# Layer 1's down projections of ten of the eleven pairs in seven products, tokens on partitions, with h turned once early

## The chip, the cores and the metric

The kernel runs on one core of one Trainium2 chip. The metric is device time in microseconds (us) for one execution. TensorE (PE) does the matmuls, VectorE (DVE), ScalarE (ACT) and GpSimd (POOL) the elementwise work, SyncE (SP) issues most DMAs. Each engine has a queue of its own and takes its instructions in order. PSUM, where matmuls add up, has 8 banks of 128 partitions by 512 fp32 values.

## The reference, cut to what matters

A decoder trunk of two layers, 512 tokens by 1024 channels, fp32. Layer 0 is a Conformer convolution module and a SwiGLU FFN, layer 1 sliding-window attention and a SwiGLU FFN, and then comes a last RMSNorm. The change lies in layer 1's FFN and what follows it:

```python
def swiglu_ffn(x, w_up, w_down):
    gate, up = jnp.split(x @ w_up, 2, axis=-1)
    return (jax.nn.silu(gate) * up) @ w_down

h = h + swiglu_ffn(rmsnorm(h, norm_ffn[l]), ffn_w_up[l], ffn_w_down[l])
return rmsnorm(h, norm_final)          # after the last layer
```

`w_up` is 1024 x 5632 and `w_down` 2816 x 1024. The kernel cuts the 2816 hidden channels into eleven "pairs" of 256.

## The kernel before, in words

**Products in three terms.** Operands are held as a high and a low part in a rounded fp32 format (fp32r): hi is a copy, lo is source minus hi. `mm3` (L346 to L352) adds hi*hi, hi*lo and lo*hi, so a product of 128x128 weights with 512 columns is three matmuls. `split` (L507) makes the parts of an activation with an ACT copy (L508) and a DVE subtraction (L509). `split_weights` (L233) does the same for weights (cast L234 on ACT, subtraction L237 on DVE).

**The weight stream.** All weights come as chunks of 128 x 1024 fp32 (512 KB) in the order of `PLAN`, through 4 buffers named `raw`. `SLOTS` lists what is to be split: a chunk, or one of the seven blocks of a pair. `advance` (L264) keeps the split three slots ahead of the matmuls; `whi` and `wlo` have 4 buffers each.

**Up projections of layer 1.** h is kept with channels on partitions, tokens along columns. Pairs 0, 2, 4, 7 and 10 are "plain" (`plain_pair`, L737): four chunks, four banks, 96 matmuls of 512 columns. Pairs 1, 3, 5, 6, 8 and 9 (`SEVENS`) go by Strassen's algorithm in Winograd's form (`ffn_up7`, L767): the 2x2 blocks A (weights: output half by input half) and B (x: input half by token half) are multiplied in seven products in place of eight. S1 to S4 are sums of weight blocks, made on POOL by `seven_sources` (L241; adds L255 to L261), T1 to T4 sums of x, made once (`Rows.sums`, L721). A product is 24 matmuls of 256 columns; its bank is added into a tile `up` by ACT, DVE and POOL (L788 to L801). Then DVE scales by the norm (L805), ACT applies silu (L807), POOL multiplies gate and up (L809), and `split` makes `hid`.

**Down projections of layer 1.** For three pairs at a time (`HALVES1`), `down_group` (L527) multiplies `hid` with 512 columns of tokens moving, and DVE adds each bank into h (L592). Pairs 9 and 10 go another way, in the tail: for each block of 128 tokens a class `Block` (L1385) turns h on PE (8 transposes, L1393) into two banks, adds the down products on top with tokens on partitions (24 matmuls, L1403), and then squares (ACT, L1408), takes 1/rms (POOL, L1414), multiplies by the gain (DVE, L1417), scales (L1425, L1427) and stores.

**The order of the work.** The kernel is written as one program; a scheduler that runs at build time sets the order on each engine, and buffers are given out from pools. The order of before: up 0-2, down 0-2, up 3-5, down 3-5, up 6-8, down 6-8, up 9, up 10, tail.

Of the kernel before, what the change touches and what calls it, by code (L numbers as in the profile page):

```python
# [14 lines left out]
ALU = mybir.AluOpType  # L15
# [20 lines left out]
HALVES1 = ((0, 3), (3, 6), (6, 9))  # L36
LAST = (9, 11)
# [18 lines left out]
SEVEN_FIRST = ("A11 B11", "S1 T1", "S3 T3", "S2 T2", "A12 B21", "S4 B22", "A22 T4")  # L56

# [5 lines left out]
def order_of(layer, pair):  # L63
    return SEVEN_FIRST if pair == SEVENS[0] else SEVEN
# [5 lines left out]

def slot_plan(plan):

    slots = []
    for i, c in enumerate(plan):
        if c[0] != "up" or not by_seven(c[1], c[2]):
            slots.append((i, None))
        elif c[3:] == (0, 0):
            slots += [(i + (3 if n else 1), (c[1], c[2], n)) for n in range(7)]
    return slots


def chunk_plan():
# [28 lines left out]
    for part in HALVES1:  # L111
        ffn(1, *part)
    for pair in range(*LAST):
        plan.extend(ups(1, pair))
    for kp in range(*LAST):
        for g in range(2):
            plan.append(("down", 1, kp, g))
# [71 lines left out]
def hybrid_trunk(ctx: ExitStack, tc: tile.TileContext, xT, W, prm_in, wdw_in, sinks, relb, onehot, fin, lead, out):  # L189
# [51 lines left out]
    def seven_sources(layer, pair, n):  # L241

        name = order_of(layer, pair)[n].split()[0]
        if name[0] == "S":
            sums[name] = sums_pool[0].tile([P, 2, 4, P], F32, tag="sum", name=uid("sum"), bufs=4)
        out = []
        for which in range(2):
            a = {f"A{m + 1}{half + 1}": raws[AT["up", layer, pair, half, which]].rearrange("p (k m c) -> p m k c", k=4, m=2)[:, m]
                 for half in range(2) if n or not half for m in range(2)}
# [3 lines left out]
            s = {k: v[:, which] for k, v in sums.items()}  # L253
# [8 lines left out]
        return out or [sums[name].rearrange("p a k c -> p (a k c)")]  # L262

    def advance():  # L264
        u = stream["use"]
        load(SLOTS[min(len(SLOTS) - 1, u + SPLIT_AHEAD - 1)][0] + 1 + DMA_AHEAD - SPLIT_AHEAD)
        while stream["split"] < min(len(SLOTS), u + SPLIT_AHEAD):
# [16 lines left out]
            for e in range(2):  # L284
                split_weights(*(w[:, e * 512:(e + 1) * 512].rearrange("p (k c) -> p k c", k=4) for w in (hi, lo)), src[e])

    def get_seven(layer, pair, n):

        advance()
        u = stream["use"]  # L290
        stream["use"] += 1
        assert SLOTS[u][1] == (layer, pair, n)
        return tuple(x.rearrange("p (a k c) -> p a k c", a=2, k=4) for x in splits.pop(u))
# [255 lines left out]
    def ffn_part(layer, part, xg, tok, rms, on_h=None, twin=False, plain=None):  # L549
        lo, hi = (HALVES0, HALVES1)[layer][part]  # L550
        hid = ffn_up7(layer, lo, hi, xg, pool7) if layer else ffn_up(layer, lo, hi, xg, tok, rms, twin, plain)
# [148 lines left out]
    class Hidden(Pairs):  # L700

        def __init__(self):
            self.per, self.q = 2, []

        def grow(self):
            self.q.append(quads.tile([P, 2, 2, 512], F32R, tag="quad", name=uid("hid")))

    class Rows:
# [12 lines left out]
        def sums(self):  # L721
# [4 lines left out]
            t1 = self.pool.tile([P, 2, 4, P], F32, tag="sum", name=uid("t1"), bufs=4).rearrange("p a k c -> p (a k c)").rearrange(  # L726
# [10 lines left out]
    def plain_pair(layer, pair, rows, hid, i):  # L737
        banks = accs(512)
        steps = None
        for half in range(2):  # L740
            for which in range(2):
                w = get("up", layer, pair, half, which)
# [14 lines left out]
        rs_bc = rows.rms.step2()  # L757
        hid.grow()
        for m in range(2):
            t1, t2 = temp(), temp()  # L760
            nc.vector.tensor_mul(t1, banks[m], rs_bc)
            nc.scalar.activation(t1, t1, AF.Silu)
            nc.vector.tensor_mul(t2, banks[2 + m], rs_bc)
            nc.gpsimd.tensor_mul(t2, t1, t2)
            split(hid[i + m], t2)

    def ffn_up7(layer, lo, hi, rows, pool):  # L767
        hid = Hidden()
        rms = rows.rms
        for pair in range(lo, hi):  # L770
            if not by_seven(layer, pair):
                plain_pair(layer, pair, rows, hid, 2 * (pair - lo))
                continue

            c = pool.tile([P, 2, 2, 2, 256], F32, tag="up", name=uid("up"), bufs=2)
            c11, c12, c21, c22 = (c[:, m, s] for m in range(2) for s in range(2))
            acc = {}
            for n, name in enumerate(order_of(layer, pair)):
                w = get_seven(layer, pair, n)
                a, b = name.split()  # L780
                x = rows.block[b]
                r = acc[a] = bank().rearrange("p (a s) -> p a s", a=2)
                for which in range(2):
                    for k in range(4):
                        mm3(r[:, which], [v[:, which, k, :] for v in w], [x[e][:, k, :] for e in range(2)],
                            which == 0 and k == 0, which == 1 and k == 3)
                if a == "A11":
                    nc.scalar.copy(c11, r)  # L788
                elif a == "S1":
                    nc.scalar.copy(c22, r)  # L790
                elif a == "S2":
                    nc.vector.tensor_add(c12, r, c11)
                    nc.vector.tensor_add(c21, acc["S3"], c12)
                    nc.gpsimd.tensor_add(c12, c12, c22)
                    nc.gpsimd.tensor_add(c22, c21, c22)
                elif a == "A12":
                    nc.vector.tensor_add(c11, r, c11)
                elif a == "S4":
                    nc.vector.tensor_add(c12, r, c12)
                elif a == "A22":  # L800
                    nc.vector.tensor_add(c21, r, c21)  # L801
            rs_bc = rms.step2().rearrange("p (s q) -> p s q", s=2).unsqueeze(2).to_broadcast([P, 2, 2, 256])
            hid.grow()
# [7 lines left out]
        return hid  # L811
# [560 lines left out]
    for part in range(len(HALVES1)):  # L1372
        ffn_part(1, part, nxt, ALL, None)

    hid = ffn_up7(1, *LAST, nxt, pool7)
    seven.close()

    res = ctx.enter_context(tc.tile_pool(name="res", bufs=2))  # L1380
    gain = res.tile([P, D], F32, tag="gain", name="gain", bufs=1)
    nc.sync.dma_start(gain, fin.to_broadcast([P, D]))
    chunks = {}

    class Block:  # L1385
        def __init__(self, b):
            self.b, self.tok = b, slice(b * P, (b + 1) * P)
            self.banks = [bank(), bank()]
            self.ss = small.tile([P, 4], F32, tag="ss", name=uid("ss"))
            self.hg = []  # L1390
            for i in range(KT):
# [40 lines left out]
    for kp in pairs:  # L1432
        for g in range(2):
            for bl in first:
                bl.down(kp, g)
                if kp == LAST[1] - 1:
                    bl.half(g)
# [36 lines left out]
```

## Time and profile before

| | us |
|---|---|
| runs before: median of 3 | 1076.69 |
| lowest, highest | 1074.96, 1078.26 |
| profiled execution, span from first to last instruction | 1073.4 |
| layer 1's FFN in it (first plain pair to the last store) | 724 to 1073 |
| down projections of three pairs, one stage | 32.6 |
| up pair, plain / seven products | 21.8 / 20.15 |
| last matmul to the end | 5.6 |

No time is listed for the profiled execution apart from its span. Rows of groups read: line, engine, operation, out<-in, shapes, count | busy us, mean ns of one | idle time before them and who ended it. Rows of timelines read: start us, length us, engine, line, operation. Rows of the chain: start us, length us, what.

### The profile page before, as it was taken

Reading aid. Unit: us, or ns where it says so; the run is one execution under the profiler, and the core shown is the slowest. Engines: PE = TensorE matmul, PEld = TensorE weight load, DVE = VectorE, ACT = ScalarE, POOL = GpSimd, SP = SyncE. Lnnn points to the kernel's source line nnn. Section 1 sums busy time; section 2 is a strip of 40 time slices with the busy share of each in tenths; the row PEclk is TensorE's granted clock in tenths of the full one; section 3 lists DMA queues with packets and bytes.
Section 4 is the critical chain, followed back from the end, with each engine's and each line's share of the span. In section 5 each row is a group of like instructions: output and inputs, shape, how many; then the busy total and the mean of one; then the engine's idle time right before and its main releaser. Section 6 shows DMA issues by size and latency. Waiting matters only on the chain.

```text
span 1073.4 us, 15809 instructions
## 1 busy us (share of the span) xinstructions
PE 1064.6 (99%) x5938; PEld 925.8 (86%) x5938; DVE 722.7 (67%) x1107; ACT 523.6 (49%) x943; POOL 434.7 (40%) x487
## 2 busy tenths in 40 slices
PE   9999999999999999999999999999999999999997
PEld 8888889999988888888888777779889898998986
DVE  3999988977777644443446566589756874866553
ACT  3887888765555333222342655475324342342333
POOL 3999998710322212111111353147352743635120
PEclk9999999999999999999999999999999999999999
DMA  9238045565555422222222211121522231324122
GB/s 353 88 100 97 2 154 200 180 233 180 182 187 191 145 98 97 99 98 98 98 87 93 76 59 66 55 77 40 177 98 79 79 138 59 138 79 137 66 73 78
DMA packets 39559, 124.45 MB, mean 116 GB/s; under 512 B 4251, under 2 KB 10556, under 8 KB 39484
## 3 DMA queue, kind: packets, MB, share of 16 engines
q1 hardware_dynamic: 38764, 122.36, 34.6%
q10 hardware_dynamic: 720, 1.10, 0.3%
q8 instruction: 46, 0.75, 0.3%
q14 instruction: 29, 0.24, 0.1%
HBM read 118.20 MB, written 5.24 MB: 115 GB/s over the span
## 4 chain that ended last, share of the span: by engine, by line
PE 96%; issue 1%; ACT 1%; DVE 1%; DMA 1%; SPq 0%; POOLq 0%; POOL 0%; DVEq 0%
PE bank L350 22%; PE bank L352 22%; PE bank L351 22%; PE bank L860 10%; PE bank L382 5%; PE bank L348 4%; PE bank L383 3%; PE bank L1403 2%; PE bank L1257 1%; PE bank L1299 1%; PE bank L1286 1%; PE bank L958 1%; PE bank L848 1%; DMA both<-in_lead_dram 1%; ACT quad L724 0%
## 5 line engine op out<-in xcount | busy, mean ns | idle before, releaser
L237 DVE TENSOR_TENSOR wlo<-raw,whi 128x1024 fp32r<-128x1024 f32 (+1 forms) x198 | 265.3, 1348 | 185.3 <-ACT whi L234 185.0
L351 PE MATMUL bank<-quad,whi 128*128 128x512 f32 (+1 forms) x1008 | 349.2, 346 | 1.0 <-DVE quad L505 1.0
L352 PE MATMUL bank<-quad,wlo 128*128 128x512 f32 (+1 forms) x1008 | 349.5, 347 | 0.0
L350 PE MATMUL bank<-quad,whi 128*128 128x512 f32 (+1 forms) x1008 | 349.4, 348 | 0.0
L234 ACT CAST whi<-raw 128x1024 fp32r<-128x1024 f32 (+1 forms) x198 | 190.3, 970 | 267.3 <-PE bank L351 209.4
L351 PEld LDWEIGHTS bank<-quad,whi 128*128 128x128 f32 x1008 | 191.1, 190 | 24.5 <-DVE quad L505 1.4
L350 PEld LDWEIGHTS bank<-quad,whi 128*128 128x128 f32 x1008 | 191.1, 190 | 24.5 <-issue 1.3
L352 PEld LDWEIGHTS bank<-quad,wlo 128*128 128x128 f32 x1008 | 191.0, 190 | 23.6 <-issue 0.6
L902 POOL TENSOR_TENSOR pr<-pr,pr 128x256 f32<-128x256 f32 x208 | 156.3, 782 | 6.7 <-ACT pr L901 6.7
L909 DVE SCALAR_TENSOR_TENSOR bank<-apad,wdw,bank 128x256 f32<-128x256 f32 x248 | 112.5, 485 | 3.4
L901 ACT ACTIVATE pr<-apad,wdw 128x256 f32<-128x256 f32 x208 | 98.2, 502 | 14.7 <-POOL pr L902 12.7
L860 PE MATMUL bank<-quad,w 128*128 128x256 f32 x448 | 98.7, 380 | 0.0
L860 PEld LDWEIGHTS bank<-quad,w 128*128 128x128 f32 x448 | 85.1, 190 | 11.7 <-DVE bank L909 0.2
L461 POOL TENSOR_TENSOR tmp<-tmp,tmp 128x256 f32<-128x256 f32 (+1 forms) x28 | 26.7, 955 | 123.1 <-ACT tmp L457 86.4
L382 PE MATMUL bank<-quad,whi 128*128 128x512 f32 x212 | 75.9, 398 | 0.0
L634 POOL TENSOR_TENSOR tmp<-tmp,tmp 128x512 f32<-128x512 f32 x12 | 17.2, 1432 | 112.0 <-DVE tmp L633 112.0
L237 DVE TENSOR_TENSOR wlo<-sum,whi 128x1024 fp32r<-128x1024 f32 x24 | 34.9, 1456 | 37.2 <-ACT whi L234 37.2
L383 PE MATMUL bank<-quad,wlo 128*128 128x256 f32 x212 | 59.4, 281 | 0.0
L351 PE MATMUL bank<-hid,whi 128*128 128x512 f32 x144 | 56.1, 390 | 0.0
L352 PE MATMUL bank<-hid,wlo 128*128 128x512 f32 x144 | 56.1, 389 | 0.0
L350 PE MATMUL bank<-hid,whi 128*128 128x512 f32 x144 | 55.8, 390 | 0.0
L352 PE MATMUL bank<-rows,wlo 128*128 128x256 f32 x192 | 54.4, 284 | 0.0
(211 smaller groups left out, 1617.0 us busy)
## 6 DMA issues: line engine op xcount, KB each, us to landing
raw<-in_W_dram SPq DMA_DIRECT2D x198, 512.0 KB, 3.6
w<-in_W_dram SPq DMA_DIRECT2D x14, 512.0 KB, 8.6
fd<-fs SPq DMA_DIRECT2D x1, 3072.0 KB, 33.5
h<-in_xT_dram SPq DMA_DIRECT2D x8, 256.0 KB, 8.5
bias<-fd SPq DMA_DIRECT2D x8, 256.0 KB, 5.0
both<-in_lead_dram SPq DMA_DIRECT2D x3, 512.0 KB, 6.3
out_dram<-hg SPq DMA_DIRECT2D x4, 256.0 KB, 2.0
out_dram<-hg ACTq DMA_DIRECT2D x4, 256.0 KB, 2.3
```

Source lines behind the costliest of these rows:

```text
L234: on_act = nc.scalar.copy(hi, src).ins
L237: latest[:] = [on_act, lo_engine[0].tensor_sub(lo, src, f32(hi)).ins]
L348: nc.tensor.matmul(out, w[0], x, start=start, stop=stop)
L350: nc.tensor.matmul(out, w[0], x[0], start=start, stop=False)
L351: nc.tensor.matmul(out, w[0], x[1], start=False, stop=False)
L352: nc.tensor.matmul(out, w[1], x[0], start=False, stop=stop)
L382: nc.tensor.matmul(first[2], first[0], first[1], start=start, stop=False)
L383: nc.tensor.matmul(second[2], second[0], second[1], start=False, stop=stop)
L860: mm = nc.tensor.matmul(self.pb[:, w * W2:(w + 1) * W2], w1_of(ct, w, k), x[k] if x else xg[k][:, tok], start=k == 0, stop=k == KT - 1)
L901: on_act = nc.scalar.mul(pr, a[:, j:j + W2], tap(j))
L902: on_pool = nc.gpsimd.tensor_add(pr, acc, pr)
L909: on_dve = nc.vector.scalar_tensor_tensor(yt if i == nd - 1 else c, src, tap(i), c if i else self.shift, op0=ALU.mult, op1=ALU.add)
```

## The change

**Down projections by seven products.** Ten pairs (0 to 9) are taken two at a time, in a "low" stage: A is `w_down` (two halves of the 1024 output columns, by the two 128-channel halves of a pair), B the hidden activations (two channel halves by two token halves). The order of stages is `STEPS1`: up 0, 1, 2, low 0, up 3, 4, low 2, up 5, 6, low 4, up 7, 8, low 6, up 9, 10, low 8, then pair 10's own down projection in the tail. So seven-product up pairs stand right ahead of low 4 (pair 6), of low 6 (pair 8), and next to each other (5, 6).

**Tokens on partitions.** The stationary operand is now a 128x128 piece of the activations, and 512 columns of weights move. One product is 12 matmuls (two token blocks, two pairs, three terms). Products add up in PSUM along three chains, `x` (A11, S2, S3, A22), `z` (S1, S4) and `y` (A12), each of two banks that are read after every product and then added to further.

**h turned once.** `flip` transposes h between the seven products of pair 1 (32 transposes on PE, 8 copies on ACT); h holds tokens on partitions from there on. The norm's scale is applied per token when a bank is added into h, so `up` is no longer scaled and DVE scales the gate alone.

**Forms.** `forms_of` makes from a pair's gated activations the four blocks B11, B12, B21, B22 and T1 to T4 (four POOL subtractions of 128x256, in place) and splits seven eighths of 2048 columns (1792) with two ACT copies and two DVE subtractions. Odd pairs keep the low part in the pool `form`, since 11 `quad` buffers would not do.

**The tail** has 12 matmuls a block for 32 matmuls and transposes; DVE scales the bank and adds h to it first, into an SBUF tile `room`, and the square and the gain work from there.

**Others.** In plain pairs DVE multiplies gate and up (POOL before). Down weights get S1 to S4 on POOL as the up weights do. `dynamic_dma_scratch_size` is 2048.

```diff
+LAST = FT // 2 - 1
+STEPS1 = [("up", 0), ("up", 1), ("up", 2), ("low", 0)]
+for _p in range(3, LAST, 2):
+    STEPS1 += [("up", _p), ("up", _p + 1), ("low", _p - 1)]
+SEVEN_LOW = ("A11 B11", "S1 T1", "S2 T2", "A12 B21", "S3 T3", "S4 B22", "A22 T4")
+def lows(pair):
+    return [("down", 1, kp, g) for g in range(2) for kp in (pair, pair + 1)]
...
-            rs_bc = rms.step2().rearrange("p (s q) -> p s q", s=2).unsqueeze(2).to_broadcast([P, 2, 2, 256])
-            hid.grow()
-            for m in range(2):
-                nc.vector.tensor_mul(c[:, m], c[:, m], rs_bc)
-                gate = c[:, m, :, 0, :]
-                nc.scalar.activation(gate, gate, AF.Silu)
-                t = temp()
-                nc.gpsimd.tensor_mul(t.rearrange("p (s q) -> p s q", s=2), gate, c[:, m, :, 1, :])
-                split(hid[2 * (pair - lo) + m], t)
+        rs_bc = rows.rms.step2().rearrange("p (s q) -> p s q", s=2)
+        for m in range(2):
+            gate = c[:, m, :, 0, :]
+            nc.vector.tensor_mul(gate, gate, rs_bc)
+            nc.scalar.activation(gate, gate, AF.Silu)
+            nc.gpsimd.tensor_mul(gate, gate, c[:, m, :, 1, :])
...
+    def forms_of(c, pool, odd):
+        f = c.rearrange("p m s w q -> p (m s w) q")
+        hi = quads.tile([P, 8, 256], F32R, tag="quad", name=uid("fhi"))
...
+        for t, a, b in (("T1", "B12", "B11"), ("T3", "B22", "B12"), ("T2", "B22", "T1"), ("T4", "B21", "T2")):
+            nc.gpsimd.tensor_sub(f[:, FORM[t]], f[:, FORM[a]], f[:, FORM[b]])
+        for part in (slice(0, 2), slice(3, 8)):
+            split((hi[:, part], lo[:, part]), f[:, part])
...
+    def low_pairs(pair, forms, rs):
+        chains = {}
+        for n, name in enumerate(order_of("low", pair)):
+            whi, wlo = get_seven("low", pair, n)
+            a, b = name.split()
+            chain, g, s = CHAINS[a]
+            first = chain not in chains
+            if first:
+                chains[chain] = [bank() for _ in range(2)]
+            for t, out in enumerate(chains[chain]):
+                for e in range(2):
+                    xh, xl = (f[:, FORM[b], t * P:(t + 1) * P] for f in forms[e])
+                    ws = slice(e * 512, (e + 1) * 512)
+                    for i, (x, w) in enumerate(((xh, whi), (xh, wlo), (xl, whi))):
+                        nc.tensor.matmul(out, x, w[:, ws], start=first and e == 0 and i == 0, stop=e == 1 and i == 2,
+                                         skip_group_check=True)
+                to, scale = rows_of(g, 2 * s + t), rs[:, 2 * s + t:2 * s + t + 1]
+                src = out.rearrange("p (i c) -> p i c", i=4)
+                if a == "A12":
+                    m = temp()
+                    nc.scalar.mul(m, out, scale)
+                    nc.gpsimd.tensor_add(to, to, m.rearrange("p (i c) -> p i c", i=4))
+                else:
+                    nc.vector.scalar_tensor_tensor(to, src, scale, to, op0=ALU.mult, op1=ALU.add)
...
+    def flip():
+        t, g = next(flips)
+        b = bank()
+        for i in range(4):
+            nc.tensor.transpose(b[:, i * P:(i + 1) * P], h[g * 4 + i][:, t * P:(t + 1) * P], ident)
+        nc.scalar.copy(rows_of(g, t), b.rearrange("p (i c) -> p i c", i=4))
...
+            nc.vector.scalar_tensor_tensor(v.rearrange("p (i c) -> p i c", i=4), acc.rearrange("p (i c) -> p i c", i=4), rs,
+                                           rows_of(g, b), op0=ALU.mult, op1=ALU.add)
+            nc.scalar.activation(temp(), v, AF.Square, accum_out=ss[:, g:g + 1])
```

More of the change, by code (lines that the diff above doesn't have):

```diff
@@ L252, in seven_sources @@
                 continue
-            s = {k: v[:, which] for k, v in sums.items()}
             if name == "S1":
@@ L1370, in hybrid_trunk @@
                 nxt = Rows("ffn1", pool7)
[L1372 to L1391, printed above, removed]
-                c = (i % 4) * P
-                nc.tensor.matmul(self.banks[i // 4][:, c:c + P], h[i][:, self.tok], ident, is_transpose=True,
-                                 start=i % 4 == 0, stop=False)
-        def down(self, kp, g):
-            if (kp, g) not in chunks:
-                chunks[kp, g] = get("down", 1, kp, g)
-            whi, wlo = chunks[kp, g]
-            for k in range(2):
-                a = cut(hid[2 * (kp - LAST[0]) + k], self.tok)
-                for n, (x, w) in enumerate(((a[0], whi), (a[0], wlo), (a[1], whi))):
-                    nc.tensor.matmul(self.banks[g], x, w[:, k, :], start=False, stop=kp == LAST[1] - 1 and k == 1 and n == 2)
-        def half(self, g):
-            ss, b = self.ss, self.banks[g]
-            sq = res.tile([P, 512], F32, tag="sq", name=uid("sq"))
-            nc.scalar.activation(sq, b, AF.Square, accum_out=ss[:, g:g + 1])
```

241 lines of the change are left out of this document (132 added, 109 removed).

## The prediction

> **What bounds the kernel now.** I read the page's busy times and chain first, then the chain in order of time, the groups of instructions, the busy time by stretch, and the timelines of VectorE (DVE) and GpSimd (POOL).
>
> ```profile
> span 1073.4 us, 15809 instructions
> ...
> PE 1064.6 (99%) x5938; PEld 925.8 (86%) x5938; DVE 722.7 (67%) x1107; ACT 523.6 (49%) x943; POOL 434.7 (40%) x487
> ...
> PEclk9999999999999999999999999999999999999999
> ...
> PE 96%; issue 1%; ACT 1%; DVE 1%; DMA 1%; SPq 0%; POOLq 0%; POOL 0%; DVEq 0%
> ```
>
> TensorE (PE) is busy 99% of the span, and 96% of the chain that ended last is PE. So fewer matmuls are worth their pace, as long as the other engines keep feeding PE. The pace is not the mean of a group:
>
> ```profile
> L351 PE MATMUL bank<-hid,whi 128*128 128x512 f32 x144 | 56.1, 390 | 0.0
> 1042.41 1.75 PE bank L1393 x16
> 1044.16 10.94 PE bank L1403 x48
> ```
>
> The first row (groups) gives 390 ns for a matmul over 512 columns, but matmuls overlap. In the chain, 48 of them take 10.94 us: 0.228 us each. I use 0.228; with 390 ns every saving would come out 1.7 times too large. The form of L1403 (activations stationary, 512 weight columns moving) is the one the new products use.
>
> ```profile
> 756.36:778.15 21.79, 21.79 (x99) 18.03 (x97) 15.02 (x15) 8.75 (x12) 6.34 (x5) 1.00 0.53 175
> 778.15:810.79 32.64, 32.64 (x146) 27.04 (x144) 17.33 (x17) 7.18 (x9) 13.77 (x9) 1.00 0.24 81
> 852.73:872.88 20.15, 20.15 (x169) 20.15 (x168) 15.61 (x17) 9.58 (x14) 5.03 (x3) 1.00 0.27 96
> ```
>
> These stretches are a plain up pair (21.79 us), the down projections of three pairs (32.64), and an up pair by seven products (20.15, so 2.88 a product). Columns: length, then busy PE, PEld, DVE, ACT, POOL, granted clock. PE has no idle time in any. The sums of a seven-product pair run on POOL in the stage before it (13.77 us in the down stage, 5.03 in its own).
>
> **What the change removes.** The order of instructions has 60 fewer 128x512 matmuls (2488 for 2548) and equal counts of every other form: two pairs' down projections take 84 for 96, five times. 60 x 0.228 = **13.7 us**. A low stage (that is what I call the seven down products of two pairs) lasts 84 x 0.228 = 19.15 us, a product 2.73. The 32 transposes move from the tail to pair 1 at the same price (1.75 / 16 = 0.11 each). Up to pair 1 of layer 1 all five queues stand in the same order.
>
> **What it adds beside PE.** A low stage splits 7 weight slots where the two pairs had 4, with 8 POOL sums of 128x512, 14 evacuations of a bank (12 on DVE, 2 on ACT and POOL) for 5.3, and for each pair 4 POOL differences of 128x256. Their prices:
>
> ```profile
> 842.26 1.78 DVE L509 TENSOR_TENSOR hid<-tmp,hid 128x512 fp32r<-128x512 f32 x1
> 843.97 2.31 DVE L237 TENSOR_TENSOR wlo<-sum,whi 128x1024 fp32r<-128x1024 f32 x1
> 846.20 0.68 DVE L761 TENSOR_TENSOR tmp<-bank,rsbc 128x512 f32<-128x512 f32 x1
> 859.69 1.23 DVE L237 TENSOR_TENSOR wlo<-sum,whi 128x1024 fp32r<-128x1024 f32 x1 [1.44 <-ACT whi L234]
> 1045.89 0.68 DVE L509 TENSOR_TENSOR hid<-tmp,hid 128x512 fp32r<-128x512 f32 x1
> ```
> ```profile
> 841.75 1.74 POOL L255 TENSOR_TENSOR sum<-raw,raw 128x512 f32<-128x512 f32 x1
> 843.45 1.74 POOL L261 TENSOR_TENSOR sum<-raw,sum 128x512 f32<-128x512 f32 x1
> 845.15 2.28 POOL L257 TENSOR_TENSOR sum<-sum,raw 128x512 f32<-128x512 f32 x1
> 847.51 1.30 POOL L261 TENSOR_TENSOR sum<-raw,sum 128x512 f32<-128x512 f32 x1
> L257 POOL TENSOR_TENSOR sum<-sum,raw 128x512 f32<-128x512 f32 x11 | 20.8, 1889 | 0.5
> L592 DVE TENSOR_TENSOR h<-bank,h 128x512 f32<-128x512 f32 x24 | 16.1, 686 | 6.1 <-PE bank L352 6.1
> ```
>
> A DVE operation with two SBUF inputs takes 0.68 us alone and 1.78 while POOL works; a POOL sum takes 1.30 alone and 1.74 to 2.28 beside DVE. They take turns: POOL starts every 1.70 us with a 512-wide DVE operation between, and a 1024-wide one stretches that to 2.36 (845.15 to 847.51). So 512 columns cost DVE about 0.6 of the turn and POOL 1.1. A DVE operation that reads a bank keeps 0.68 (L592: 686 ns over 24), so the 12 evacuations cost 0.69 each and take no turn; as scalar_tensor_tensor they are unmeasured at this width, and I let them be 0.6 to 0.8.
>
> In halves of 512 columns, then: a seven-product up stage has DVE 14 (weights) + 2 (gates) + 3.5 (splits of the forms) and POOL 8 + 2 + 2 + 2 (forms, halves of 256), so 19.5 x 0.6 + 14 x 1.1 = 27.1 us of turns in 20.15 us of PE. A low stage: 14 x 0.6 + 10 x 1.1 = 19.4 in 19.15. A plain pair: 11.5 x 0.6 + 2 x 1.1 = 9.1 in 21.8. The only place with two dear stages and no cheap one between is pair 5, pair 6, low 4 (73.6 in 59.5), and pair 8, low 6, pair 9 (73.6 in 59.5). Each is 14 over. Against that stand three weight slots made ahead (3 x 2.88 = 8.6) and the forms of its last pair, which can fall into the plain pair behind (2 x 1.1 + 3.5 x 0.6 = 4.3). So 1 us of stall at least in each, if the queues never stand in each other's way.
>
> The Trainium skill, page "SBUF — State Buffer", section "SBUF: two separate sides", has the same as a rule: DVE with two SBUF inputs and a reading GpSimd operation hold one port pair by turns, for a whole instruction. By it the 27.1 stands; by plain overlap the stage would need only 15.4 (POOL's part) and nothing would be over. The 1.70 us turns agree with the rule.
>
> **The path of low 4 and low 6.** Here the weights of a low stage follow a seven-product pair, whose raw chunks stay in use until its last product (A22) is split.
>
> ```profile
> raw<-in_W_dram SPq DMA_DIRECT2D x198, 512.0 KB, 3.6
> ACT whi L234 <- PE bank L351: 109.3, 49, 4.4
> L234 ACT CAST whi<-sum 128x1024 fp32r<-128x1024 f32 x24 | 25.1, 1046 | 50.6 <-PE bank L351 41.2 <-issue 8.2 <-POOL sum L255 1.2
> ```
>
> The casts wait for PE to free a buffer (109.3 us), so A22's split starts when PE ends the pair's S1 product; call that time 0. The split ends at about 2.4 (a cast of half a slot, 0.6, then DVE's 0.68 to 1.78), SP issues the chunks for row half 2, they land 3.6 later, at 6.0. S1 of the low stage needs them, and it is its second product. PE gets there after S2, A12, S4, A22 (4 x 2.88) and A11 (2.73), at 14.25. In POOL's built order S1 is complete with the 4th operation in low 4 and the 5th in low 6 (sums of S2 and S3 and an addition of the pair stand between), S2 four and five operations later. With 1.55 us an operation, between 1.30 and the 1.89 of L257, then 1.05 for the cast and 1.23 for DVE:
> - low 6: S1 at 6.0 + 7.75 + 2.3 = 16.05, PE stalls about 1.3 (two matmuls need the cast alone); S1 ends at 18.3; S2 is ready at 16.05 + 7.75 = 23.8; less four matmuls it can do first (0.9), a stall of 4.6.
> - low 4: S1 at 14.5, no stall; it ends at 17.0; S2 at 20.7, a stall of 2.8.
>
> Sum **8.7 us**. With 1.30 an operation it is 4.2, with 1.89 it is 15. Behind the waiting cast on ACT stand the next casts, and behind DVE's split the evacuations; both are in the sum. Low 0, 2 and 8 follow a plain pair, whose chunks come free one by one, three slots of 5.5 us ahead: nothing. Pair 1 gets 8 ACT copies for the turned h and needs 16 banks in 24 us: 0 to 3, I take 1.0 for this and small waits. Fewer scratch bytes for dynamic DMA: every queue of the page that moves a kernel's data is issued by SP or ACT, so 0. The load of the gains now stands on SP ahead of the last two chunks and waits for a matmul of pair 9, long past: 0.
>
> **The tail.**
>
> ```profile
> 1067.79 0.60 ACT L1408 ACTIVATE sq<-bank 128x512 f32<-128x512 f32 x1 [2.03 <-PE bank L1403]
> 1069.34 0.72 ACT L1427 ACTIVATE hg<-hg,rs 128x512 f32<-128x512 f32 x1 [0.85 <-POOL rs L1414]
> 1068.75 0.55 POOL L1414 TENSOR_TENSOR rs<-ss,mhalf 128x1 f32<-128x1 f32 x1 [5.78 <-DVE ss L1412]
> 1068.59 0.69 DVE L1417 TENSOR_TENSOR hg<-bank,gain 128x512 f32<-128x512 f32 x1
> 1069.39 0.48 DVE L1425 TENSOR_SCALAR hg<-hg,rs 128x512 f32<-128x512 f32 x1
> ```
>
> Now 5.6 us lie between the last matmul (1067.8) and the end: square, 1/rms, scale, store. The new tail puts a DVE operation (0.69) ahead of each square, and DVE has four operations of 0.6 and one of 0.4 a block, 3.0 us, for 12 matmuls of 2.7: it ends the tail. By its built order the last scale ends 4.2 us after the last matmul, then 3.3 as now: 7.5, **+1.9** (0.7 if only the one operation counts, 3 with waits).
>
> **Sum**, against the span of 1073.4, which lies 3.3 under the median 1076.69 of the runs; I carry the difference over: -13.7 + 8.7 + 1.0 + 1.9 = -2.1, so **1074.6 us**. About 3.2 us (0.3%) is what a measurement here can tell from no change.
>
> **Rivals.**
> - *The cover holds.* The sums run as fast as alone and raw chunks land early; stalls 0 to 4.2: 1064.9 to 1069.1, say 1067. For it: no PE idle in any stretch above, though turns are taken there too. Against it: no stage of before has sums due right behind a seven-product pair.
> - *The turns become the bound.* Half of the cover (12.9 in each place) is lost since the queues are in order: 28 - 13 = 15 of stall, and 4 where low 0 and low 2 meet pairs 3 and 5 (27.1 + 19.4 in 39.3, 7 over each): -13.7 + 1.9 + 19 = +7.2, 1084. It decides from 15 us of stall on. For it: L257 at 1.89 instead of 1.30. Against: four plain pairs that need 9.1 of 21.8.
> - *The clock drops.* In every slice PEclk is 9, and the stretches above have 1.00. If it halved for one product behind each stall, each would lose 2.73: 1080. The Trainium skill, "TensorE: Matmul & The Clock Gate", section "What's actually happening", halves it after an idle window of about 3.4 us; by that, an estimate, 1.7 would be lost in each place. No run here shows it.
> - *It does not do what it says*: excluded, the built order has the 60 matmuls less.
>
> **Chances.** Forecast 0.44 (1070 to 1079); cover holds 0.23; turns bound 0.27; clock 0.06. Faster by over 0.3%: 0.23 and a good third of the forecast (stalls under 7.6), 0.39. Within: 0.29. Slower: 0.27 and the clock, 0.32. The range reaches from inside the first rival to the second's price: 1066 to 1084; it leaves out the best of the one and the worst of the other.
>
> **What would show it.** PE's 128x512 matmuls 60 fewer at 0.228; low 0, 2 and 8 near 19.2 us, low 4 near 22 and low 6 near 25, with PE's idle time put down to the split (wlo) or cast (whi) of S2; POOL's mean sum over 1.5; a tail with DVE last. Wrong, if low 4 and low 6 last 19 to 20, or if stalls stand in low 0, 2 and 8 or inside the seven-product pairs.

## The result and the profile after

The changed kernel takes 1090.87 us (median of 4 runs, 1089.23 to 1091.58), the kernel before 1077.47 beside it (1074.96 to 1079.25). The ratio is 1.0125, with a 95% interval of 1.0108 to 1.0142: some 13 us slower. I had forecast 1074.6, at most 1084. The profiled run of the changed kernel took 1090.52, with a span of 1088.7, against a span of 1073.4 before. A run lasts 1.8 us longer than its span, so 1073.4 answers to some 1075.2, one of the short runs of before; that is why the spans lie 15.3 us apart and the medians 13.4.

The page of the changed kernel, the lines that answer to those shown of before:

```profile
span 1088.7 us, 15932 instructions
...
PE 1063.3 (98%) x5878; PEld 920.5 (85%) x5878; DVE 778.2 (71%) x1181; ACT 554.5 (51%) x991; POOL 544.4 (50%) x567
...
PEclk9999999999999999999999999989999998999999
...
PE 86%; POOL 5%; DVE 4%; issue 2%; ACT 1%; DMA 1%; SPq 0%; POOLq 0%; DVEq 0%; ACTq 0%
```

Two things are new. PE has 60 matmuls fewer (5878 for 5938), but is hardly less busy (1063.3 for 1064.6 us), and PEclk, which was 9 everywhere, has slices of 8. And POOL and DVE now hold 9% of the chain, where before POOL had 0% and DVE 1%.

The stretches in which PE runs the first 72 matmuls of each low stage, in the order low 0, 2, 4, 6, 8 (busy PE, PEld, DVE, ACT, POOL, then granted clock):

```profile
786.50:803.14 16.64, 16.64 (x75) 13.73 (x74) 15.27 (x20) 7.85 (x11) 10.42 (x10) 1.00 0.38 127
847.71:864.35 16.64, 16.64 (x75) 13.72 (x74) 14.78 (x19) 7.85 (x11) 11.03 (x10) 1.00 0.37 128
911.07:936.14 25.07, 20.63 (x75) 15.18 (x74) 19.46 (x22) 10.58 (x14) 21.85 (x15) 0.86 0.20 63
980.63:1003.80 23.17, 18.78 (x76) 14.52 (x75) 19.94 (x18) 10.54 (x15) 22.67 (x16) 0.93 0.24 72
1049.71:1066.36 16.65, 16.65 (x74) 13.73 (x73) 15.18 (x22) 8.76 (x12) 3.74 (x2) 1.00 0.17 64
```

Low 0, 2 and 8 run at 16.64 / 72 = 0.231 us a matmul (0.229 from one start to the next), with no idle time. Low 4 and low 6 take 8.4 and 6.5 us more. In low 4 PE is idle for 25.07 - 20.63 = 4.4 us, and nearly all of the rest is the clock (0.86). POOL, busy for 10 to 11 of 16.6 us in low 0 and 2, is busy for 22 of 25.1 and of 23.2 us in low 4 and 6.

The waits of PE from layer 1's FFN on, in the changed kernel (us in total, times, longest):

```profile
PE bank L857 <- ACT whi L244: 7.7, 3, 3.7
PE bank L857 <- DVE wlo L247: 1.1, 2, 0.7
PE bank L857 <- DVE h L866: 1.1, 1, 1.1
PE bank L368 <- ACT whi L244: 1.0, 1, 1.0
PE bank L369 <- DVE quad L523: 1.0, 1, 1.0
PE bank L370 <- DVE wlo L247: 0.8, 1, 0.8
PE bank L489 <- DVE tmp L479: 0.5, 1, 0.5
```

L857 is a low product: 9.9 us of waits, all in low 4 (4.4) and low 6 (5.5). L368 and L370 are products of up pair 6, 1.8. The lines with quad L523 and tmp L479 stand in before as well (1.0 and 0.5). So 11.7 us of new waits.

The stretches of the changed kernel in which the clock is halved (the clock is the third number from the end of a row):

```profile
725.39:732.22 6.83, 6.83 (x21) 5.67 (x21) 6.83 (x5) 2.09 (x2) 6.13 (x4) 0.50 0.16 30
899.47:902.88 3.41, 3.41 (x18) 3.41 (x17) 3.41 (x3) 3.06 (x5) 3.33 (x3) 0.50 0.00 0
916.53:919.94 3.41, 2.96 (x7) 2.17 (x7) 2.25 (x4) 0.00 (x0) 3.41 (x3) 0.50 0.00 0
923.36:926.77 3.41, 3.38 (x9) 2.07 (x8) 3.41 (x4) 2.56 (x4) 3.33 (x3) 0.50 0.00 0
991.63:995.04 3.41, 3.02 (x7) 2.44 (x8) 3.41 (x4) 1.44 (x2) 3.41 (x3) 0.50 0.14 22
```

They last 3.41 us or twice that, and each of the last four stands behind a wait: in pair 6, twice in low 4, and in low 6. At half the clock 3.41 us do the work of 1.7. The first lies behind two holes (1.0 and 0.5 us) near pair 0 that the kernel before has too.

The sum of the profiled runs, 15.3 us between the spans:

| | us |
|---|---|
| 60 matmuls fewer, 0.228 each | -13.7 |
| waits in pair 6, low 4, low 6 | +11.7 |
| four halved windows behind them, 1.7 each | +6.8 |
| the halved window near pair 0 | +3.4 |
| tail, 8.7 us after the last matmul (1080.0) for 5.6 | +3.1 |
| layer 0 and attention, where nothing was changed | +1.75 |
| left over | +2.3 |

Of the left over, 0.9 is the pace: from one start to the next a low product's matmul takes 0.229 us, one of the old down projections 0.227, over 420 of them. The rest wasn't followed further. The 1.75, and the halved window near pair 0, differ from trace to trace: that window is halved in 9 of the 14 traces of this study and not in 5, with the same two holes in all.

### The profile page after: what moved, and what is told of

Same layout as the page of the kernel before. It is cut to its first block, busy times and chain, and to the rows that moved or that the text cites. A ratio compares the mean times of both kernels' runs of the same rounds, so it can differ in the third digit from the quotient of the medians.

```text
span 1088.7 us, 15932 instructions
## 1 busy us (share of the span) xinstructions
PE 1063.3 (98%) x5878; PEld 920.5 (85%) x5878; DVE 778.2 (71%) x1181; ACT 554.5 (51%) x991; POOL 544.4 (50%) x567
## 4 chain that ended last, share of the span: by engine, by line
PE 86%; POOL 5%; DVE 4%; issue 2%; ACT 1%; DMA 1%; SPq 0%; POOLq 0%; DVEq 0%; ACTq 0%
PE bank L368 17%; PE bank L369 17%; PE bank L370 17%; PE bank L915 10%; PE bank L857 6%; PE bank L400 5%; PE bank L366 4%; PE bank L401 3%; DVE wlo L247 2%; PE bank L1312 1%; PE bank L1354 1%; PE bank L1341 1%; POOL sum L270 1%; POOL sum L272 1%; PE bank L1013 1%
## 5 line engine op out<-in xcount | busy, mean ns | idle before, releaser
L247 DVE TENSOR_TENSOR wlo<-raw,whi 128x1024 fp32r<-128x1024 f32 (+1 forms) x208 | 259.3, 1257 | 156.5 <-ACT whi L244 156.0
L368 PE MATMUL bank<-quad,whi 128*128 128x512 f32 (+1 forms) x1008 | 350.5, 349 | 0.0
L370 PE MATMUL bank<-quad,wlo 128*128 128x512 f32 (+1 forms) x1008 | 349.9, 347 | 0.0
L244 ACT CAST whi<-raw 128x1024 fp32r<-128x1024 f32 (+1 forms) x208 | 186.6, 912 | 234.0 <-PE bank L369 169.2
L368 PEld LDWEIGHTS bank<-quad,whi 128*128 128x128 f32 x1008 | 191.9, 190 | 24.9 <-issue 1.6
L370 PEld LDWEIGHTS bank<-quad,wlo 128*128 128x128 f32 x1008 | 191.5, 190 | 24.0 <-issue 0.6
L247 DVE TENSOR_TENSOR wlo<-sum,whi 128x1024 fp32r<-128x1024 f32 x44 | 64.7, 1470 | 37.1 <-ACT whi L244 37.0
L479 POOL TENSOR_TENSOR tmp<-tmp,tmp 128x256 f32<-128x256 f32 (+1 forms) x28 | 26.7, 954 | 123.3 <-ACT tmp L475 86.6
L244 ACT CAST whi<-sum 128x1024 fp32r<-128x1024 f32 x44 | 46.0, 1047 | 83.2 <-POOL sum L270 48.1
L857 PE MATMUL bank<-whi,fhi 128*128 128x512 f32 x140 | 53.7, 405 | 8.8 <-ACT whi L244 7.7
L857 PE MATMUL bank<-wlo,fhi 128*128 128x512 f32 x140 | 57.4, 410 | 1.2 <-DVE wlo L247 1.1
L1331 POOL TENSOR_SCALAR sc<-sc,sm 128x256 f32<-128x256 f32 (+1 forms) x64 | 31.2, 506 | 52.9 <-DVE sm L1329 52.6
```

Of the source, the lines that this page charges most:

```text
L244: on_act = nc.scalar.copy(hi, src).ins
L247: latest[:] = [on_act, lo_engine[0].tensor_sub(lo, src, f32(hi)).ins]
L368: nc.tensor.matmul(out, w[0], x[0], start=start, stop=False)
L370: nc.tensor.matmul(out, w[1], x[0], start=False, stop=stop)
L857: nc.tensor.matmul(out, x, w[:, ws], start=first and e == 0 and i == 0, stop=e == 1 and i == 2, skip_group_check=True)
```

## Experiments

Two theories stood at first. The **path**: the sums of a low stage come late, because a seven-product pair in front frees its raw chunks late (so the forecast put it). The **turns**: where two dear stages adjoin a low stage, DVE and POOL need the shared port for longer than PE's work lasts. And for the clock: it falls because PE is idle, or because of something else in the change.

**Seven-product pairs only ahead of plain ones.**

```diff
-SEVENS = (1, 3, 5, 6, 8, 9)
+SEVENS = (1, 3, 5, 7, 9)
```

> Five up pairs by seven products (1, 3, 5, 7, 9) in place of six, so that a plain pair stands ahead of every low stage and no two seven-product pairs adjoin. PE has 24 more matmuls of 512 columns for 168 of 256: 21.8 - 20.15 = +1.6 us. In the changed kernel PE waited 1.8 us inside pair 6, 4.4 in low 4 and 5.5 in low 6, and the clock was halved four times for 3.41 us right behind those waits (6.8 us lost): 18.5 in all. Path theory (the sums of a low stage come late because its raw chunks are freed late by a seven-product pair) and turns theory (POOL and DVE have more turns than time where dear stages adjoin) both expect that all of it goes: about 1090.9 - 18.5 + 1.6 = 1074, and 1071 if the halved clock near pair 0 (3.4 us) goes as well. Rival (a low stage is too dear by itself, wherever it stands): waits of 4 us or more stay in low 4 and low 6, 1085 or more.

Measured 1071.15 us against 1076.4 before: 0.995 (0.9932 to 0.9969). PE from 940 to 1060 us of this kernel, the stretch in which low 6 and low 8 run (the latter but for its end), and all its waits from the FFN's first product on:

```profile
940.00:1060.00 120.00, 120.00 (x637) 103.75 (x635) 94.25 (x111) 51.32 (x74) 72.24 (x50) 1.00 0.28 93
```
```profile
PE bank L368 <- DVE tmp L775: 1.8, 1, 1.8
```

No wait in any low stage, and no halved window before PE's last matmul. The 1.8 is in pair 1. So a low stage isn't too dear by itself; what stands in front of it decides. Both theories expected that.

**Another order of the low products.** (One line: `SEVEN_LOW` = A11, A12, S1, S2, S3, S4, A22.)

> Order of the products of a low stage: A11, A12, S1, S2, S3, S4, A22, so A12, which needs no POOL sum, comes second and S1 third, one product (2.73 us) later. Path theory: the wait for S1 and S2 shrinks by 2.73 in low 4 (4.4 to 1.7) and in low 6 (4.4 to 1.7), and two or three halvings of the clock (1.7 each) go with it: about 1081. The wait inside pair 6 (1.8) stays. Turns theory: the amount of work on POOL and DVE is the same, so the wait comes at S2, S3 or later in the stage: 1088 to 1092.

Measured 1093.78 against 1076.4: 1.0158 (1.0139 to 1.0178), above the turns' range (1088 to 1092) and far from the path's 1081. The waits in low 4 and 6 stay (9.2 us by the profile), and 3.5 come up in the pair behind low 6. To be needed later didn't help: against the path.

**A12 on DVE alone.**

```diff
-                if a == "A12":
-                    m = temp()
-                    nc.scalar.mul(m, out, scale)
-                    nc.gpsimd.tensor_add(to, to, m.rearrange("p (i c) -> p i c", i=4))
-                else:
-                    nc.vector.scalar_tensor_tensor(to, src, scale, to, op0=ALU.mult, op1=ALU.add)
+                nc.vector.scalar_tensor_tensor(to, src, scale, to, op0=ALU.mult, op1=ALU.add)
```

> The two A12 banks of a low stage are added into h by DVE straight from the bank (0.74 us each) in place of an ACT copy (0.69) and a POOL addition of two SBUF operands (1.58): POOL loses 3.2 us a stage, DVE gains 1.5 that takes no turn on the port. Turns theory: the wait in low 4 and low 6 falls by up to 3 each, and behind it the clock: 1080 to 1086. Path theory: the additions of A12 stand behind S1 and S2 of their own stage, so less than 2 us of change, 1089 to 1091.

Measured 1088.94 against 1076.4: 1.0111 (1.009 to 1.0132), which overlaps the changed kernel's 1.0108 to 1.0142. Taken as forecast, this fits the path (1089 to 1091) and not the turns (1080 to 1086): POOL has 3.2 us less to do in a stage, and the waits in low 4 and low 6 are 10.7 us for 9.9. But the turns' figure had left out when the work falls. In the changed kernel POOL's two additions of A12 begin at 932.4 in low 4, behind its last wait (to 923.0), and at 1001.1 in low 6, behind the main one (to 990.1). So the run is inconclusive.

**The late chunks made those that need fewer sums.**

```diff
...
-    return [("down", 1, kp, g) for g in range(2) for kp in (pair, pair + 1)]
+    return [("down", 1, kp, g) for g in (1, 0) for kp in (pair, pair + 1)]
...
-SEVEN_LOW = ("A11 B11", "S1 T1", "S2 T2", "A12 B21", "S3 T3", "S4 B22", "A22 T4")
+SEVEN_LOW = ("S1 T1", "A11 B11", "S2 T2", "A12 B21", "S3 T3", "S4 B22", "A22 T4")
```

> Chunks of a low stage come with the second output half first (A21, A22, then A11, A12), and the products go S1, A11, S2, A12, S3, S4, A22. So the two chunks that come early are those S1 needs, and the late ones are needed by A11 (no POOL sum) and S2. Behind the late landing stand two POOL sums (S2) in place of four (S1, S2). Path theory: the wait in low 4 and low 6 falls by two POOL operations, 3 us each, and one or two halvings of the clock go: about 1081 to 1083. Turns theory: 1088 to 1092.

Measured 1090.21 against 1076.4: 1.013 (1.0109 to 1.0151), no gain, in the range of the turns. Low 6's waits fell to 1.8, low 4's rose to 6.1, and low 0 and low 8 got 1.8 and 1.4. Again the waits move and don't go.

**A shorter DVE operation in the place of the split.**

```diff
+        if seven:
+            nc.vector.tensor_copy(lo, f32(hi)[:, 0:1].to_broadcast(lo.shape) if len(lo.shape) == 2 else f32(hi)[:, :, 0:1].to_broadcast(lo.shape))
+            return
...
```

This kernel and the next leave out the low part of the weights in all slots of seven products.

> The changed kernel, but the low part of the weights of every seven-product slot is not computed: DVE writes the first column of the high part over all columns, so it reads one operand from SBUF in place of two; every other instruction stays. Turns theory (a DVE operation with two SBUF inputs and a POOL sum take turns on one port): POOL's sums go from a mean of about 1.7 to about 1.3 us, DVE's splits to their time alone, and the waits in pair 6, low 4 and low 6 and the halved clock behind them go: about 1090.9 - 18.5 = 1072. Rival (too many instructions on POOL and DVE, or late sums, whatever the port does): POOL's sums keep their 1.7, 1088 to 1092. If DVE's new operation turns out much shorter than 0.69 for 512 columns, it is POOL's own length that tells the two apart.

Measured 1073.51 against 1076.35: 0.9968 (0.9953 to 0.9983). The waits of PE are 3.9 us, and but for the window near pair 0 no window is halved. But POOL's own length, which was to tell the theories apart, lies in between. DVE's new operation and the dearest POOL sum (groups, from the FFN on):

```profile
L246 DVE CAST wlo<-whi 128x512 fp32r<-128x512 f32 x64 | 46.2, 742 | 13.3 <-ACT whi L244 12.4
```
```profile
L279 POOL TENSOR_TENSOR sum<-raw,sum 128x512 f32<-128x512 f32 x21 | 36.5, 1743 | 0.4
```

The copy takes 742 ns on average, though 410 at the least, and POOL's 82 sums still average 1.55 us: beside POOL, the copy with one SBUF operand is lengthened as well, and the sums with it, only less. The Trainium skill, page "SBUF — State Buffer", section "SBUF: two separate sides", counts DVE's two-port modes among those that lock the port pair. The lengthened copies fit that if the copy runs in such a mode, which no run here shows by itself. So this run doesn't tell the port from DVE's amount of work.

**DVE's splits off the port, and not shorter.**

```diff
+        if seven:
+            if not fixed:
+                fixed.append(bank())
+                nc.vector.memset(fixed[0], 0.0)
...
+                for j in range(src.shape[1] // 512):
+                    nc.vector.tensor_sub(lo[:, j * 512:(j + 1) * 512], f32(hi)[:, j * 512:(j + 1) * 512], fixed[0])
+            return
...
```

> The changed kernel, but the low part of the weights of every seven-product slot is not computed: DVE subtracts a PSUM bank of zeros from the high part, 512 columns at a time, so it has one operand in SBUF and one in PSUM, at the length of the evacuations (0.69 for 512, 1.38 in place of 1.21 for 1024). So DVE has as much work as before, a little more, but its splits leave the port. Turns theory: POOL's sums fall from a mean of 1.64 to at most 1.4, and the waits in pair 6, low 4 and low 6 and the halved clock go: 1072 to 1075, with up to 2 more since one bank is taken away. Rival (DVE's amount of work, not the port): POOL's sums keep 1.6, waits as before, 1088 to 1094.

Measured 1069.44 against 1076.26: 0.9941 (0.9927 to 0.9954), below the range of the turns theory. Splits and sums, from the FFN on, first of the changed kernel, then of this one:

```profile
L247 DVE TENSOR_TENSOR wlo<-raw,whi 128x512 fp32r<-128x512 f32 x64 | 60.4, 975 | 5.5 <-ACT whi L244 5.5
L247 DVE TENSOR_TENSOR wlo<-sum,whi 128x1024 fp32r<-128x1024 f32 x43 | 63.5, 1476 | 37.1 <-ACT whi L244 37.0
```
```profile
L276 POOL TENSOR_TENSOR sum<-raw,sum 128x512 f32<-128x512 f32 x21 | 39.0, 1859 | 0.5
L272 POOL TENSOR_TENSOR sum<-sum,raw 128x512 f32<-128x512 f32 x21 | 35.9, 1713 | 0.4
```
```profile
L255 DVE TENSOR_TENSOR wlo<-whi,bank 128x512 fp32r<-128x512 f32 x115 | 73.8, 681 | 34.6 <-ACT whi L246 34.0
```
```profile
L288 POOL TENSOR_TENSOR sum<-raw,sum 128x512 f32<-128x512 f32 x21 | 32.5, 1547 | 0.5
L284 POOL TENSOR_TENSOR sum<-sum,raw 128x512 f32<-128x512 f32 x21 | 27.9, 1330 | 0.5
```

A split of 512 columns takes 681 ns with an operand in PSUM (670 to 691 in all its places), where it took 975 on average and up to 1787 with both in SBUF. L284's sums fall from 1713 (then L272) to 1330 ns; the mean of all sums is 1.39 us for 1.64. DVE's work alone has not become less (two operations of 681 in the place of one over 1024 columns, which takes 1210 at the least). The waits in pair 6, low 4 and low 6 fall from 11.7 to 0.8 us, and no window is halved before the last matmul. The instructions on POOL are the same, with six seven-product pairs and all. One thing beside the port differs: raw chunks and POOL's sums come free earlier, since DVE doesn't read them. In the changed kernel POOL waited for no sum to be split between 860 and 1020 us, so the chunks are left. POOL's first sum of low 4 and of low 6 in this kernel (timeline, idle time in brackets):

```profile
897.32 1.94 POOL L282 TENSOR_TENSOR sum<-raw 128x512 f32<-128x512 f32 x1 [3.09 <-DMA raw<-in_W_dram]
959.49 1.29 POOL L282 TENSOR_TENSOR sum<-raw 128x512 f32<-128x512 f32 x1 [9.78 <-DMA raw<-in_W_dram]
```

Low 4 begins at 904.4 here and low 6 at 966.6. So in low 6 the first sum begins 7.1 us ahead of its stage, where in the changed kernel it was 6.3, after much the same wait for a chunk; even so PE's waits there fall from 5.5 to 0.2 us. In low 4 it begins 7.1 us ahead for 1.9, so there the earlier chunk can have a share. With that reserve for pair 6 and low 4, the turns on the port are the cause. The next run weighs the chunks alone.

**Five raw chunks.** (The pool of raw chunks has 5 buffers in place of 4, the odd pairs' low forms 7 blocks in place of 8, and `dynamic_dma_scratch_size` is 1024 for 2048.)

> The changed kernel with five raw chunks in place of four (room for it by cutting the unused eighth of the low forms). The third chunk of a low stage, the first that S1 needs, can then land before the seven-product pair in front ends; the fourth as before. If it matters that POOL waits for raw chunks at the border (3.0 us of idle time ahead of low 4, 1.4 ahead of low 6), the waits fall by 1 to 2 us in each place, and the time to 1086 to 1089. If the turns of POOL and DVE alone set them: 1090 to 1092.

Measured 1091.08 against 1076.26: 1.0137 (1.0123 to 1.015), no gain. The waits are 11.2 us, low 6's down to 2.4, with new ones in pairs 5 and 6. The first sum of low 4 now begins 15.2 us ahead of its stage, that of low 6 22.7. Then POOL waits for DVE instead: 5.2 and 4.0 us ahead of two sums of low 6, until DVE has split earlier ones. So a chunk more moves the waits and doesn't lessen them, and the path as forecast doesn't set their size. The fourth chunk of a stage came late here too (the second S1 sum begins 1.9 us ahead of low 4 and 4.1 ahead of low 6); six chunks had no room and weren't tried.

**The low stages' sums on DVE.** (The four lines of `seven_sources` go by `nc.vector` for low stages.)

> The S sums of the low stages (8 of 128x512 a stage) on DVE in place of POOL. Turns theory: 0.6 of the turn in place of 1.1 each, so 4 us less a low stage; what is over in each of the two places falls from 14 to 10, and the waits there by about half: 1080 to 1084. If POOL's amount of work alone were the bound, all waits would go: 1072. If DVE's own time becomes the bound (14 x 0.6 + 8 x 0.68 + 14 x 0.74 and more in 19.15 us), waits appear in low 0, 2 and 8 as well: 1090 or more.

Measured 1084.68 against 1076.35: 1.0081 (1.0052 to 1.011). Lower than the changed kernel by 0.4%, near 5 us, though the two intervals just touch: the way of the turns, but just above their range, and far from the 1072 for POOL's amount of work. Low 6's waits fell from 5.5 to 2.2. Those of low 4 did not (5.3).

**The adjoining pairs put elsewhere.** (`SEVENS` = 1, 3, 5, 7, 9, 10.)

> Pairs 1, 3, 5, 7, 9 and 10 by seven products: six again, but the one place where dear stages adjoin is now pair 9, pair 10, low 8. Turns theory: the waits of 4 to 6 us and one or two halvings of the clock (1.7 each) that stood in low 6 now stand in pair 10 or low 8, and nowhere else: the alternating kernel's 1071.2 - 1.6 + 6 to 9 = 1075.6 to 1078.6. Rival (adjoining does not matter, the stretch from pair 5 to low 6 was disturbed by something else): 1069.5.

Measured 1082.39 against 1076.35: 1.0057 (1.0036 to 1.0078). The waits of PE:

```profile
PE bank L857 <- ACT whi L244: 4.6, 2, 2.6
PE bank L857 <- DVE wlo L247: 1.8, 3, 0.6
PE bank L368 <- ACT whi L244: 1.0, 1, 1.0
PE bank L370 <- DVE wlo L247: 0.8, 1, 0.8
```

Low 4 and low 6 have none now. Low 8, which had none in the changed kernel, has 6.3, and pair 10 has 1.9; two windows are halved behind them. The place follows the adjoining pairs, at 8.2 us a place for the 4 to 6 that I had put down, which is why the time lies above the range. The path, too, would put waits behind pair 10, so this run speaks against the rival alone.

**Holes in the kernel before.**

```diff
+                if pair in HOLES and which == 0:
+                    x = rows.x[half * 4][0]
+                    for _ in range(HOLES[pair][half]):
+                        nc.vector.tensor_copy(x, f32(x))
...
```

In these pairs the order of the matmuls is changed as well, so that the chunks on both sides of a hole use the copied tile.

> The kernel before, with eight holes made on purpose in PE's work: in the plain pairs 2, 4, 7 and 10, between the two chunks of a half, DVE copies one activation tile onto itself 1, 2, 3, 4, 5, 2, 3 and 1 times (0.48 us each), and PE has to wait for it. Holes of about 0.5 + 0.48 n: 1.0, 1.5, 1.9, 2.4, 2.9, 1.5, 1.9, 1.0, some 14 us in all. Theory that idle time of PE halves the clock in the next window of 3.41 us when about 1.5 us of a window are idle: four to six halvings behind the longer holes, 1.7 us each: 1076.5 + 14 + 7 to 10 = 1097 to 1101. Rival (the halved clock of the changed kernel comes from something else in it): no halvings, 1090.

Measured 1092.79 against 1076.35: 1.0152 (1.0117 to 1.0187). Only two holes came about, in pairs 4 and 7, but long ones, 5.87 and 6.92 us, so the time lies below the range that stood for eight. Two stretches of this kernel, which begin inside the holes:

```profile
847.38:854.21 6.83, 5.08 (x12) 4.09 (x13) 4.86 (x8) 0.63 (x1) 1.32 (x1) 0.50 0.25 77
949.78:956.61 6.83, 3.12 (x7) 2.48 (x8) 6.00 (x8) 0.64 (x1) 2.28 (x2) 0.50 0.24 79
```

The clock, 1.00 in the kernel before, halves for 6.83 us at both, and nowhere else before the tail. So idle time of PE is enough; the change's own instructions aren't needed. The two places cost some 8.5 us each for holes of 5.9 and 6.9; part of each hole lies in the halved stretch itself. How long a short hole must be, this run can't say.

**The tail's gain on POOL**, with alternating pairs.

```diff
-            nc.vector.tensor_mul(o, v, gain[:, g * 512:(g + 1) * 512])
+            (nc.vector if g else nc.gpsimd).tensor_mul(o, v, gain[:, g * 512:(g + 1) * 512])
```

> The alternating kernel (pairs 1, 3, 5, 7, 9 by seven products), and in the tail POOL multiplies the first half of a block by the gain, so that DVE has 2.6 us a block in place of 3.3 against PE's 2.7. If DVE's backlog makes the tail's 8.7 us: the last addition of h follows the last matmul at once, and the time falls by 0.7 to 1.5, to 1069.7 to 1070.5. If the chain behind the last matmul (square, 1/rms, scale, store) sets it: 1071, no change.

Measured 1070.37 against 1076.26: 0.9945 (0.9931 to 0.9958), the same as the alternating kernel within the intervals. The time lies in the range that was put down for DVE's backlog, but the trace decides otherwise: from the last matmul to the end lie 8.54 us, with the gain on DVE 8.75, and the last addition of h still ends 1.5 us after that matmul. So DVE's gain is not what makes the tail longer.

**A correct way off the port.**

```diff
+        if via:
...
+            for j in range(2):
+                part = slice(j * 512, (j + 1) * 512)
+                nc.scalar.copy(fixed[0], src[:, part])
+                nc.vector.tensor_sub(lo[:, part], fixed[0], f32(hi)[:, part])
+            return
```

> The changed kernel with its six seven-product pairs, computing all that the reference asks: for the slots that are sums (S1 to S4, four of seven), ACT also copies the sum, 512 columns at a time, into one PSUM bank, and DVE subtracts the high part from that bank, so that 8 of the 14 halves of a stage take no turn on the port. Turns theory: a seven-product stage then has 27.1 - 8 x 0.6 = 22.3 us of turns, a low stage 14.6, the two places 59.2 in 59.5: nearly all waits and the halved clock go, 1070 to 1075, as far as the one bank keeps up (0.62 + 0.69 and two hand-overs a half, 3.2 us a slot where a product lasts 2.73 to 2.88). Rival (ACT's 5 us more a stage and the queue behind one bank take the place of the turns): waits at the casts, 1078 to 1088.

Measured 1092.19 against 1077.43: 1.0144 (1.0126 to 1.0162). The first waits of ACT from the FFN on:

```profile
ACT bank L252 <- DVE wlo L253: 35.2, 34, 4.1
ACT whi L246 <- POOL sum L280: 27.8, 9, 5.5
```

ACT stands 35 us waiting for DVE to empty the one bank, with all the other casts queued behind. Sums on POOL get shorter (1.44 us on average), and the queue eats it. The rival was right, and priced too low (1078 to 1088).

## Why the prediction was wrong

- **The matmuls (-13.7).** Right but for 0.9: 60 fewer, at 0.229 us from one start to the next where nothing waits. PE has no wait in pair 1 for the turned h (1.0 was put down), and none that stands for the scratch or the gain's load.
- **Where the waits are.** Right for low 4 and low 6, and for none in low 0, 2 and 8. Pair 6 (1.8) was missed, and waits inside a seven-product pair were one of the forecast's own signs of being wrong. The size was 9.9 for 8.7 in the low stages (4.4 for 2.8 in low 4, 5.5 for 5.9 in low 6), 11.7 in all.
- **Why they are there.** The step "the path of low 4 and low 6" gave nearly the right size by luck, for the wrong reason: to need the sums later, to have fewer behind the late chunk, or to land a chunk earlier didn't lessen the waits. The right reason stood a paragraph higher, in the turns: 14 us over in each place. It was put aside by a cover of 12.9, as if POOL could always work ahead. It can't, as the changed kernel's timeline shows (idle time before the operation in brackets):

```profile
884.23 2.18 POOL L270 TENSOR_TENSOR sum<-raw,raw 128x512 f32<-128x512 f32 x1 [8.00 <-DVE up L805]
...
909.18 1.53 POOL L270 TENSOR_TENSOR sum<-raw 128x512 f32<-128x512 f32 x1 [3.04 <-DMA raw<-in_W_dram]
...
974.29 1.56 POOL L270 TENSOR_TENSOR sum<-raw 128x512 f32<-128x512 f32 x1 [8.77 <-DMA raw<-in_W_dram]
```

  Ahead of pair 6, of low 4 and of low 6 POOL stood idle for 8.0, 3.0 and 8.8 us, since the chunks for its next sums weren't there (ahead of the first one too: by the chain of waits a raw chunk landed at 884.1). Then the turns began, with 28 us over in the two places, and PE waited 11.7. By this estimate the cover was 16 of 26 us, between the forecast's whole and the second rival's half; that rival's waits where low 0 and 2 meet pairs 3 and 5 did not come. More chunks are not all that the cover needs: with five of them POOL went on to wait for DVE's splits.
- **The clock.** This is the step that failed and put the time outside the range: the sum has no term for it. It was a rival of its own at 0.06, priced as one product in each of two places, when it is no other case but a tax on the forecast's own waits. Holes of 1.8 (in two parts) to 3.7 us halved the clock four times (6.8 us), and the two near pair 0 once (3.4). With the waits as forecast and this tax the time would have been 1074.6 + 6.8, near 1081: the upper part of the range, and slower. What lies beyond that is the halved window near pair 0, 2.0 more of waits than was put down (11.7 for 8.7 + 1.0), the tail and what differs from trace to trace.
- **The tail.** It costs +3.1 for +1.9. Its end in the changed kernel:

```profile
1080.75 0.74 DVE L1468 SCALAR_TENSOR_TENSOR room<-bank,rs,h 128x512 f32<-128x512 f32 x1
...
1082.24 1.56 POOL L1476 TENSOR_TENSOR rs<-ss,mhalf 128x1 f32<-128x1 f32 x2 [2.10 <-DVE ss L1472]
1083.28 1.33 ACT L1483 ACTIVATE room<-room,rs 128x512 f32<-128x512 f32 x2 [1.03 <-POOL rs L1476]
```

  DVE's last addition of h ends at 1081.5, 1.5 us after the last matmul. Then two blocks are due at once: POOL has two operations (1.56 us) and ACT two scalings (1.33) where before it was one each. The last scaling ends 4.6 us after the last matmul, for 4.2 in the forecast, and from there to the end it is 4.1 us, for the 3.3 of before that the forecast had kept. That reading is from the trace; the run with the gain on POOL took one suspect out and named none.

What stays open: why low 4 kept its waits when the low sums went to DVE, and which of the 3.1 us of the tail could be had back.

## What to carry to other kernels

Add up, stage by stage, the time that DVE's operations with SBUF operands alone and POOL's take in turns, and count work ahead as cover only as far as POOL's inputs can be there. In this kernel a saving in matmuls that needs more sums paid only where such a stage had a cheap one in front of it: five seven-product pairs, spaced out, beat both kernels (0.995), six with two side by side lose (1.0125, and 1.0057 in another place). And price waits of PE that come to some 1.5 us or more within 3.4 us at themselves plus 1.7 us of halved clock.

## What the runs showed of the hardware

- **A hole needn't fill a window.** In all 14 traces the halved stretches between the start and the tail last 3.41 or 6.83 us, on a fixed grid. PE's idle time in the 3.41 us ahead (taken 0.4 us earlier than the grid, since the profile's ends of matmuls are modelled) was 1.25 us or more for each of the 30 that began, and at most 1.94 us where none did. The two overlap, so no sharp border can be given. The Trainium skill, page "TensorE: Matmul & The Clock Gate", section "What's actually happening", has the clock halved after an idle window of about 3.4 us, in a window that runs freely. The grid agrees; but the window need not be wholly idle, since a hole of 2.0 us was enough in low 4. The measurement decides.
- **Which window it falls in.** The same two holes near pair 0, 1.0 and 0.5 us, cost nothing in before and 3.4 us in the changed kernel: by the grid, they lie on both sides of a border in the one and in the same window in the other. Over all 14 traces, with the same 0.4 us, 1.25 to 1.51 us of them fall into one window in the nine that were halved, and 0.8 to 1.0 us in the five that were not.
- **An operand in PSUM.** A DVE subtraction of 512 columns takes 0.681 us with one operand in PSUM (0.691 at the most, with POOL at work beside it), and 0.975 on average, 1.787 at the most, with both in SBUF beside POOL's sums.
